# A hybrid encoder layer: early products read in place, rotary multiplications ordered behind the next job's first split, two norm products moved to VectorE

## The chip, the cores and the metric

The kernel runs on one core of a Trainium2 chip. The time is device microseconds from the start to the end of one execution; the figure of a kernel is the median of several executions. One execution is also recorded by the hardware profiler. Engines are named as in the profile: PE (TensorE: matmuls and transposes; PEld its weight loads), DVE (VectorE), ACT (ScalarE), POOL (GpSimd) and SP (SyncE, which here only issues transfers).

## The reference

One layer of an encoder trunk for 1024 tokens of width 1024, in float32:

```
x = x + 0.5 * norm(SwiGLU_1(norm(x)))                 # FFN 1, inner width 2816
u = norm(x);  rq, rk, rv, rg, nq, nk, nv, g_ret, g_na = split(u @ W_mix_in)
y_ret = (silu(rg) * headnorm(retention(rotary(rq), rotary(rk), rv))) @ W_ret_out
y_na  = neighbourhood_attention(nq, nk, nv) @ W_na_out
x = x + norm((sigmoid(g_ret) * y_ret + sigmoid(g_na) * y_na) @ W_mix_out)
x = x + 0.5 * norm(SwiGLU_2(norm(x)))                 # FFN 2
SwiGLU(x) = (silu(g) * up) @ w_out,  [g, up] = x @ w_in
rotary(x): [x1*cos - x2*sin, x1*sin + x2*cos], x1, x2 the halves of a head's 128 columns
norm(x) = x * rsqrt(mean(x*x) + 1e-6) * gain
```

## The kernel before

**Splitting.** A float32 matrix product is made of three matmuls on operands split in a high and a low part: `split` (L57) writes the high part with a cast on ACT (L62) and the low part with a subtraction on DVE (L63); `mm3` (L92) issues the three matmuls (L94, L95, L96; the third uses the low part of the stationary operand). Weight pieces come as `wraw` tiles of 128 x 1024 (four buffers, loaded through SP's queue, L73) and are split into `wh` and `wl` (eight buffers each).

**Pairs.** The large projections are done with a seven-product scheme (Strassen-Winograd) on pairs of weight tiles. One call of `Pairs.run` (L509) is a *job*: it loads the two tiles `g` and `u`, forms t1 to t4 from their halves on DVE (L525, L526, L536, L545), and makes the products p1, p6, p2, p7, p5, p4, p3 with the seven forms of x (`a11`, `s2`, `a12`, `s3`, `s1`, `a22`, `s4`). Every product is 12 matmuls into one PSUM bank. DVE adds the products up into four output tiles (`c11`, `c12`, `c21`, `c22`); `done(j)` is called when output j is complete.

**Early products.** The products of `a11` and `a12` need no t, so those of the first pairs are made before the jobs begin (`lead`, L460, and `leads`, L446). Of a *held* pair they stay in PSUM; of a *saved* pair (three in each FFN) `lead` copies both to SBUF tiles, named `lead` in FFN 1 and `g` in FFN 2, six buffers each. `run` then starts with a copy of p1 into the output tile c12 (L524) and adds p6 there (L535). In the FFNs c12 is the first half of a tile `gt` with three buffers, which `LeftFactors` (L577) later splits in place and stores to DRAM as `g0a`, `g0s` (FFN 1) or `g1a`, `g1s` (FFN 2); the stores are issued on POOL's queue (L69). FFN 1 makes the early products of a seventh pair as well, and leaves them in PSUM (tag `pt`).

**Mixer jobs.** Twelve pairs make the transposed outputs of the mixer's projection: four of neighbourhood q and k, then alternately a rotary job (rq and rk of a head; four in all) and a SiLU job (rg), then two sigmoid jobs. In a rotary job `done` calls `rotate` (L1048): two multiplications on DVE by the sine and cosine tables (L1051, L1052), a store, and two accumulating stores that swap the halves later.

**FFN output.** `ffn_out` (L689) does the seven products over 11 blocks each for 512 tokens and 512 columns at a time; a *step* is one block, 12 matmuls. When the product of `a22` ends, `p4` (L759) finishes tokens 0 to 3: the sum on DVE (L760), then `Epilogue.square` (L660): a sum of squares on ACT (L663) and a multiplication by the gain (L664), on POOL unless an engine is given. The rest of the two norms is cut into stages (`stages`, L764), which are appended to the list `later`; each following step takes one entry from its front: rstd (on POOL, L104), the residual (L674) with its sum of squares (L677), the second norm (L685), and the transposes on PE (`flip`, L133). FFN 2 has no second norm (`ep.pre` is None).

**Order.** Every engine and queue works in its own fixed order. A scheduler draws it up ahead of the run with a model of the durations: of the instructions that are ready by the model, the one written first goes first. A "NoSync" dependency (`after`, L76; `behind`, L503) fixes the order of two instructions on one engine.

Of the kernel before, what the change touches and what calls it, by code (L numbers as in the profile page):

```python
# [14 lines left out]
ALU = mybir.AluOpType  # L15
# [399 lines left out]
class Pairs:  # L415
# [2 lines left out]

    def __init__(self, c, x, srcs, held, saved=0):
        self.c, self.x, self.srcs, self.held, self.saved = c, x, srcs, held, saved  # L420
        self.begun, self.fetched, self.ready = {}, {}, {}
        self.last = None
        self.between = lambda: None

# [35 lines left out]
    def lead(self, save=None, between=(), on_pool=(), abreast=1, extra=0, early=False):  # L460

        def split(i):
            if i not in self.fetched:
                self.fetch(i)
            w = self.fetched[i]
            self.ready[i] = self.c.piece(w[:, :512])
            self.fetched[i] = [None, self.c.piece(w[:, 512:])]

        n = self.held + self.saved
        tiles = [i for i in (*range(self.held, n), *range(self.held), *range(n, n + extra)) if i not in self.begun]  # L470
        while tiles:
            group, tiles, abreast = tiles[:abreast], tiles[abreast:], 1
            for i in group:
                if i not in self.fetched:
                    self.fetch(i)
            g = [self.fetched.pop(i) for i in group]
            eng = self.c.nc.gpsimd if group[0] in on_pool else None
            tag = ("ps", 6) if group[0] < n else ("pt", 2)
            ps = [self.products("a11", [self.ready.pop(i) if i in self.ready else w[:, :512] for i, w in zip(group, g)],
                                eng, tag),  # L480
                  self.products("a12", [w[1] if isinstance(w, list) else w[:, 512:] for w in g], eng, tag)]
            if early and tiles:
                split(tiles[0])
            if between:
                f = between.pop(0)()
                if f is not None:
                    between.append(f)
            for i, *pair in zip(group, *ps):
                if self.held <= i < n:
                    sb = [save(), save()]  # L490
                    for a, b in zip(sb, pair):
                        for p, s in self.pieces(a):
                            self.c.nc.scalar.copy(p, b[:, s])
                    pair = sb
                self.begun[i] = pair

    @staticmethod
    def pieces(a):
        a = a if isinstance(a, list) else [a]
        n = 512 // len(a)  # L500
        return [(p, slice(j * n, (j + 1) * n)) for j, p in enumerate(a)]

    def behind(self, e):  # L503

# [1 line left out]
            self.c.tc.add_manual_dep(e.ins, self.last.name, mybir.DependencyInfo(  # L506
                mybir.DependencyClass.NoSync, mybir.DependencyReason.DATA), reason="order")

    def run(self, i, out, done):  # L509

        c, nc = self.c, self.c.nc
        tt = nc.vector.tensor_tensor
        g, u = (c.raw(a) for a in self.srcs[i])
        b11, b21, b12, b22 = g[:, :512], g[:, 512:], u[:, :512], u[:, 512:]

        t1, t3, t4 = b11, b12, b21
        t2 = c.wpool.tile([P, 512], F32, tag="t2", name="t2", bufs=2)

        begun = self.begun.get(i)
        p1 = begun[0] if begun else self.product("a11", b11)  # L520
        c11, c12 = out(0), out(2)
        u1 = c12 if begun else c11
        for p, s in self.pieces(p1):
            nc.scalar.copy(u1[:, s], p)  # L524
        self.behind(tt(t1, b12, b11, ALU.subtract))  # L525
        tt(t2, b22, t1, ALU.subtract)  # L526
        p6 = self.product("s2", t2)
        if not begun:
            tt(c12, p6, c11, ALU.add)
        p2 = begun[1] if begun else self.product("a12", b21)  # L530
        for p, s in self.pieces(p2):
            tt(c11[:, s], p, u1[:, s], ALU.add)  # L532
        done(0)
        if begun:
            tt(c12, p6, c12, ALU.add)  # L535
        self.behind(tt(t3, b22, b12, ALU.subtract))  # L536
        p7 = self.product("s3", t3)
        c21 = out(1)
        self.last = tt(c21, p7, c12, ALU.add).ins
        p5 = self.product("s1", t1)  # L540
        c22 = out(3)
        tt(c22, p5, c21, ALU.add)
        tt(c12, p5, c12, ALU.add)
        done(3)
        tt(t4, b21, t2, ALU.subtract)  # L545
        p4 = self.product("a22", t4)
        tt(c21, p4, c21, ALU.add)
        done(1)
        p3 = self.product("s4", b22)
        self.end = tt(c12, p3, c12, ALU.add).ins  # L550
        done(2)
# [137 lines left out]
def ffn_out(c, tiles, q, blocks, w_out, gl, ep, tail, side={}):  # L689
# [3 lines left out]
    nc = c.nc  # L693
    NK = FT // 2
    tt, add = nc.vector.tensor_tensor, nc.gpsimd.tensor_tensor
# [62 lines left out]

    def p4(u, b):  # L759
        tt(q[3][:, u], b, q[3][:, u], ALU.add)  # L760
        ep.square(u, 0, q[3][:, u], b)
        later.extend(stages(u, (q[3][:, u], q[2][:, u])))

    def stages(t, halves):  # L764
        g = ep.steps(t, xs[t], halves)

        f = []
        return [lambda: next(g), lambda: next(g)] + [
            lambda: f.append(next(g)), lambda: f[0](*(("ps", 6) if i < 6 else ("pt", 2)))] * (ep.pre is not None)

    def p2(u, b):
# [273 lines left out]
            nc.vector.tensor_scalar(q, q, RET_SCALE, None, ALU.mult)  # L1045


def rotate(c, t, x, cos, sin, dst):  # L1048

    tt = c.nc.vector.tensor_tensor  # L1050
    tt(t, x, sin, ALU.mult)  # L1051
    tt(x, x, cos, ALU.mult)  # L1052
    c.store(dst, x)

    def swap():
        c.nc.gpsimd.dma_start(dst[0:64], t[64:128], accum_op=ALU.add)
        c.nc.gpsimd.dma_start(dst[64:128], t[0:64], accum_op=ALU.add)
    return swap
# [159 lines left out]
def trunk_layer(ctx: ExitStack, tc, x, xt, g1a, w1i, w1o, g1b, gma, wmt, wnv, wrv, logits, dtab, rope, bias,  # L1218
                wro, wno, wmo, gmb, g2a, w2i, w2o, g2b, out):
    nc = tc.nc  # L1220
# [5 lines left out]
    c = Core(tc, const, wpool, psum, dram)  # L1226
# [29 lines left out]
    with tc.tile_pool(name="fin1", bufs=1, reuse_waits="tile") as fp:  # L1256
# [23 lines left out]
    ep = pool(ep_stack, "ep1")  # L1280
    g1 = pool(g_stack, "gl11")
    b11, b12, b21, b22 = ([p.tile([P, 4, 512], F32, tag="x", name="x", bufs=n) for p, n in q] for q in (
        ((x0pool, 4),) * 3, ((x1pool, 2), (x1pool, 2), (x0pool, 4)), ((spool, 8),) * 3, ((spool, 8),) * 3))
    q = [p.tile([P, 4, 512], F32, tag="x", name="q", bufs=n) for p, n in ((ep, 2), (ep, 2), (spool, 8), (spool, 8))]
# [72 lines left out]
    with tc.tile_pool(name="pa", bufs=1, reuse_waits="tile") as pa:  # L1357
        evpool[:] = [pa]
        fill.drain()
        swaps = []  # L1360

        def half():
            return pa.tile([P, 512], F32, tag="ev", name="ev", bufs=6)
# [6 lines left out]
        for i, (_, _, f, g, fn) in enumerate(jobs):  # L1370
# [6 lines left out]
            def done(j):  # L1377
                h = j % 2
                dst = (f, g)[j // 2][:, h * 512:(h + 1) * 512]
                while swaps:  # L1380
                    swaps.pop()()
                if fn == "rotary":
                    swaps.append(rotate(c, half(), parts[j], *tabs[h], dst))
                    return
                if fn is not None:
                    nc.scalar.activation(parts[j], parts[j], fn)
                c.store(dst, parts[j])
            mx.run(i, part, done)
            if i == 2:
                x1pool = pool(x1_stack, "x1b", "right")  # L1390
                a21[:] = [x1pool.tile([P, 4, 512], F32R, name=f"a21{q}") for q in "hl"]
# [251 lines left out]
```

## Time and profile before

| | |
|---|---|
| median of 3 runs | 2256.15 us (2255.41 to 2257.74) |
| the profiled execution | 2254.28 us, span 2252.5 us |
| PE busy | 2196.9 us, 98% of the span |
| DVE busy | 1637.6 us, 73% |
| ACT busy | 985.0 us, 44% |
| POOL busy | 581.7 us, 26% |
| granted TensorE clock, mean | 0.994 |

How to read the rows. In a timeline: start in us from the span's start, duration, engine, line, operation, output tile <- input tiles, shape, count of merged instructions, and in brackets how long the engine stood idle before it and what released it. Matmuls overlap, so their durations are longer than the distance of their starts. A row of waits gives who waited for whom, total us, number of times, longest. A row of the windows gives the busy time of each engine in a stretch of the span, then the granted clock as a share of full speed, the share of the DMA engines and GB/s.

### The profile page before, as it was taken

The numbers are of one execution on the slowest core, as the hardware profiler recorded it, in microseconds if no ns is written. First come the engines' busy times: TensorE is split into PE (matmuls) and PEld (weight loads), VectorE is DVE, ScalarE is ACT, GpSimd is POOL, SyncE is SP. The second block draws the span as 40 slices with busy tenths as digits, with TensorE's granted clock in tenths as the row PEclk, the third lists the DMA queues.
The fourth block names the chain that finished last, engine by engine and source line by source line (L and its number), as shares of the span: only waits on it lengthen the run. The fifth ranks groups of instructions, "written<-read, shape, count | busy, mean of one in ns | idle before, by whom it ended". The sixth has DMA issues, their size and how long they took to land.

```text
span 2252.5 us, 29976 instructions
## 1 busy us (share of the span) xinstructions
PE 2196.9 (98%) x10200; PEld 1824.7 (81%) x10200; DVE 1637.6 (73%) x2911; ACT 985.0 (44%) x2041; POOL 581.7 (26%) x756
## 2 busy tenths in 40 slices
PE   6899999999998999999999999999999999999998
PEld 5678888888786887888888888888887888888886
DVE  7898878765459857759885678553899887876444
ACT  5444434332345322249785665422544343433232
POOL 1121212158521112311101222111112121215942
PEclk9999999999999999999999999999999999999999
DMA  6354434497555555557665466686446443449865
GB/s 252 131 176 161 169 140 156 180 395 297 196 184 188 173 175 142 140 165 252 195 217 176 152 221 234 246 305 227 146 145 219 141 178 131 163 158 365 291 227 180
DMA packets 155464, 449.89 MB, mean 200 GB/s; under 512 B 19632, under 2 KB 50480, under 8 KB 153200
## 3 DMA queue, kind: packets, MB, share of 16 engines
q1 hardware_dynamic: 112800, 311.36, 40.9%
q0 software_dynamic: 42512, 136.62, 16.7%
q8 instruction: 81, 1.33, 0.2%
q14 instruction: 71, 0.58, 0.1%
HBM read 302.93 MB, written 149.17 MB: 201 GB/s over the span
## 4 chain that ended last, share of the span: by engine, by line
PE 82%; DVE 6%; ACT 4%; issue 4%; DMA 2%; POOL 2%; POOLq 0%; SPq 0%; DVEq 0%; ACTq 0%
PE ps L96 26%; PE ps L95 25%; PE ps L94 25%; PE pt L95 1%; PE pt L96 1%; PE pt L94 1%; POOL rstd L104 1%; ACT wh L62 1%; DMA wraw<-in_dram 1%; ACT s L937 1%; DVE wl L63 1%; DMA qraw<-nq 1%; DVE s L933 0%; PE pt L133 0%; ACT pth L62 0%
## 5 line engine op out<-in xcount | busy, mean ns | idle before, releaser
L63 DVE TENSOR_TENSOR wl<-wraw,wh 128x512 fp32r<-128x512 f32 x472 | 314.7, 683 | 61.0 <-ACT wh L62 60.7
L62 ACT CAST wh<-wraw 128x512 fp32r<-128x512 f32 x476 | 272.9, 618 | 159.3 <-PE ps L95 57.5
L94 PE MATMUL ps<-wh,g 128*128 128x512 f32 x548 | 214.1, 391 | 0.4 <-DVE tmp L231 0.4
L95 PE MATMUL ps<-wl,g 128*128 128x512 f32 x548 | 213.6, 390 | 0.0
L96 PE MATMUL ps<-wh,g 128*128 128x512 f32 x548 | 213.3, 389 | 0.0
L567 ACT ACTIVATE c<-c 128x512 f32<-128x512 f32 x88 | 55.4, 632 | 195.1 <-DVE c L532 101.6
L63 DVE TENSOR_TENSOR wl<-w,wh 128x512 fp32r<-128x512 f32 x77 | 77.0, 1018 | 86.2 <-ACT wh L62 86.0
L63 DVE TENSOR_TENSOR wl<-x,wh 128x512 fp32r<-128x512 f32 x77 | 79.7, 1051 | 75.1 <-ACT wh L62 73.7
L94 PEld LDWEIGHTS ps<-wh,g 128*128 128x128 f32 x548 | 102.9, 188 | 21.9 <-DVE tmp L231 0.7
L95 PEld LDWEIGHTS ps<-wl,g 128*128 128x128 f32 x548 | 102.9, 188 | 21.3 <-DVE wl L63 0.5
L96 PEld LDWEIGHTS ps<-wh,g 128*128 128x128 f32 x548 | 102.9, 188 | 21.3
L94 PE MATMUL ps<-a11h,wh 128*128 128x512 f32 x276 | 111.3, 403 | 7.7 <-ACT wh L62 7.7
L62 ACT CAST wh<-t 128x512 fp32r<-128x512 f32 x58 | 36.0, 621 | 184.0 <-DVE t L526 183.9
L96 PE MATMUL ps<-a11h,wl 128*128 128x512 f32 x276 | 109.6, 398 | 6.2 <-DVE wl L63 6.1
L95 PE MATMUL ps<-a11l,wh 128*128 128x512 f32 x276 | 109.9, 398 | 0.1
L96 PE MATMUL ps<-a22h,wl 128*128 128x512 f32 x280 | 109.1, 390 | 0.6 <-DVE wl L63 0.6
L94 PE MATMUL ps<-a22h,wh 128*128 128x512 f32 x280 | 109.7, 392 | 0.0
L94 PE MATMUL ps<-a12h,wh 128*128 128x512 f32 x276 | 108.7, 394 | 0.5 <-ACT wh L62 0.3
L95 PE MATMUL ps<-a22l,wh 128*128 128x512 f32 x280 | 109.1, 390 | 0.0
L95 PE MATMUL ps<-a12l,wh 128*128 128x512 f32 x276 | 107.5, 390 | 0.0
L96 PE MATMUL ps<-a12h,wl 128*128 128x512 f32 x276 | 107.5, 389 | 0.0
L94 PE MATMUL ps<-s2h,wh 128*128 128x512 f32 x232 | 91.8, 396 | 7.5 <-ACT wh L62 7.5
(427 smaller groups left out, 6287.2 us busy)
## 6 DMA issues: line engine op xcount, KB each, us to landing
wraw<-in_dram SPq DMA_DIRECT2D x204, 512.0 KB, 4.6
g<-g0s SPq DMA_DIRECT2D x44, 512.0 KB, 4.2
g<-g1s SPq DMA_DIRECT2D x44, 512.0 KB, 4.8
g<-g0a SPq DMA_DIRECT2D x33, 512.0 KB, 3.3
g<-g1a SPq DMA_DIRECT2D x33, 512.0 KB, 4.4
g0s<-gth POOLq DMA_DIRECT2D x44, 256.0 KB, 4.7
g0s<-cmb POOLq DMA_DIRECT2D x44, 256.0 KB, 3.7
g1s<-gth POOLq DMA_DIRECT2D x44, 256.0 KB, 4.7
```

The costliest lines, as they stand in the source:

```text
L62: self.done = [nc.scalar.copy(h, src).ins, (eng or nc.vector).tensor_tensor(l, src, hf, ALU.subtract).ins]
L63: (eng or nc.vector).tensor_tensor(l, src, hf, ALU.subtract).ins]
L94: mm(ps, a[0], b[0], start=start, stop=False)
L95: mm(ps, a[0], b[1], start=False, stop=False)
L96: mm(ps, a[1], b[0], start=False, stop=stop)
L104: self.nc.gpsimd.tensor_tensor(r[:, :n], ms, self.mhalf[:, :n], ALU.pow)
L567: nc.scalar.activation(gate[j], gate[j], AF.Silu)
L937: nc.scalar.activation(s[:, e], s[:, e], AF.Exp, bias=st[:, 2 + e:3 + e], accum_out=st[:, 4 + e:5 + e])
```

## The change

`lead` marks the saved pairs (`kept`) and copies each product whole. In `run`, a kept pair's p1 is read where it was saved: there is no copy into c12, and both additions take the saved tile. A job that is called with `nxt` loads the next job's `g` tile and splits its first half right after the product p5 is issued; the subtraction of that split is named `ahead`, and the next job uses the pieces (`ready`) instead of splitting anew. Rotary jobs set `nxt`, and the first multiplication of `rotate` for the outputs 3, 1 and 2 is ordered behind `ahead` on DVE. In `ffn_out` of FFN 1, the multiplication by the gain in `p4` is done on DVE for tokens 0 and 1, and an empty entry is put in front of token 0's last two stages in `later`. The helper `pieces` goes.

```diff
--- before.py
+++ after.py
@@ -418,7 +418,7 @@
 
     def __init__(self, c, x, srcs, held, saved=0):
         self.c, self.x, self.srcs, self.held, self.saved = c, x, srcs, held, saved
-        self.begun, self.fetched, self.ready = {}, {}, {}
+        self.begun, self.fetched, self.ready, self.kept = {}, {}, {}, set()
         self.last = None
         self.between = lambda: None
 
@@ -489,16 +489,10 @@
                 if self.held <= i < n:
                     sb = [save(), save()]
                     for a, b in zip(sb, pair):
-                        for p, s in self.pieces(a):
-                            self.c.nc.scalar.copy(p, b[:, s])
+                        self.c.nc.scalar.copy(a, b)
                     pair = sb
+                    self.kept.add(i)
                 self.begun[i] = pair
-
-    @staticmethod
-    def pieces(a):
-        a = a if isinstance(a, list) else [a]
-        n = 512 // len(a)
-        return [(p, slice(j * n, (j + 1) * n)) for j, p in enumerate(a)]
 
     def behind(self, e):
 
@@ -506,38 +500,42 @@
             self.c.tc.add_manual_dep(e.ins, self.last.name, mybir.DependencyInfo(
                 mybir.DependencyClass.NoSync, mybir.DependencyReason.DATA), reason="order")
 
-    def run(self, i, out, done):
+    def run(self, i, out, done, nxt=False):
 
         c, nc = self.c, self.c.nc
         tt = nc.vector.tensor_tensor
-        g, u = (c.raw(a) for a in self.srcs[i])
+        g = self.fetched.pop(i) if i in self.fetched else c.raw(self.srcs[i][0])
+        u = c.raw(self.srcs[i][1])
         b11, b21, b12, b22 = g[:, :512], g[:, 512:], u[:, :512], u[:, 512:]
 
         t1, t3, t4 = b11, b12, b21
         t2 = c.wpool.tile([P, 512], F32, tag="t2", name="t2", bufs=2)
 
         begun = self.begun.get(i)
-        p1 = begun[0] if begun else self.product("a11", b11)
+        p1 = begun[0] if begun else self.product("a11", self.ready.pop(i, b11))
         c11, c12 = out(0), out(2)
-        u1 = c12 if begun else c11
-        for p, s in self.pieces(p1):
-            nc.scalar.copy(u1[:, s], p)
+        u1 = p1 if i in self.kept else c12 if begun else c11
+        if u1 is not p1:
+            nc.scalar.copy(u1, p1)
         self.behind(tt(t1, b12, b11, ALU.subtract))
         tt(t2, b22, t1, ALU.subtract)
         p6 = self.product("s2", t2)
         if not begun:
             tt(c12, p6, c11, ALU.add)
         p2 = begun[1] if begun else self.product("a12", b21)
-        for p, s in self.pieces(p2):
-            tt(c11[:, s], p, u1[:, s], ALU.add)
+        tt(c11, p2, u1, ALU.add)
         done(0)
         if begun:
-            tt(c12, p6, c12, ALU.add)
+            tt(c12, p6, u1, ALU.add)
         self.behind(tt(t3, b22, b12, ALU.subtract))
         p7 = self.product("s3", t3)
         c21 = out(1)
         self.last = tt(c21, p7, c12, ALU.add).ins
         p5 = self.product("s1", t1)
+        if nxt:
+            self.fetch(i + 1)
+            self.ready[i + 1] = c.piece(self.fetched[i + 1][:, :512])
+            self.ahead = c.done[1].name
         c22 = out(3)
         tt(c22, p5, c21, ALU.add)
         tt(c12, p5, c12, ALU.add)
@@ -758,14 +756,15 @@
 
     def p4(u, b):
         tt(q[3][:, u], b, q[3][:, u], ALU.add)
-        ep.square(u, 0, q[3][:, u], b)
+        ep.square(u, 0, q[3][:, u], b, None, nc.vector if u < 2 and ep.pre is not None else None)
         later.extend(stages(u, (q[3][:, u], q[2][:, u])))
 
     def stages(t, halves):
         g = ep.steps(t, xs[t], halves)
+        wait = [None] * (t == 0 and ep.pre is not None)
 
         f = []
-        return [lambda: next(g), lambda: next(g)] + [
+        return [lambda: next(g), lambda: next(g)] + wait + [
             lambda: f.append(next(g)), lambda: f[0](*(("ps", 6) if i < 6 else ("pt", 2)))] * (ep.pre is not None)
 
     def p2(u, b):
@@ -1045,10 +1044,10 @@
             nc.vector.tensor_scalar(q, q, RET_SCALE, None, ALU.mult)
 
 
-def rotate(c, t, x, cos, sin, dst):
+def rotate(c, t, x, cos, sin, dst, behind):
 
     tt = c.nc.vector.tensor_tensor
-    tt(t, x, sin, ALU.mult)
+    c.after(tt(t, x, sin, ALU.mult).ins, behind)
     tt(x, x, cos, ALU.mult)
     c.store(dst, x)
 
@@ -1380,12 +1379,12 @@
                 while swaps:
                     swaps.pop()()
                 if fn == "rotary":
-                    swaps.append(rotate(c, half(), parts[j], *tabs[h], dst))
+                    swaps.append(rotate(c, half(), parts[j], *tabs[h], dst, [] if j == 0 else [mx.ahead]))
                     return
                 if fn is not None:
                     nc.scalar.activation(parts[j], parts[j], fn)
                 c.store(dst, parts[j])
-            mx.run(i, part, done)
+            mx.run(i, part, done, fn == "rotary")
             if i == 2:
                 x1pool = pool(x1_stack, "x1b", "right")
                 a21[:] = [x1pool.tile([P, 4, 512], F32R, name=f"a21{q}") for q in "hl"]
```

## The prediction

> **What bounds the kernel now.** I read the page first, then who TensorE (PE) waited for, then the timeline around each wait.
>
> ```profile
> span 2252.5 us, 29976 instructions
> ...
> PE 2196.9 (98%) x10200; PEld 1824.7 (81%) x10200; DVE 1637.6 (73%) x2911; ACT 985.0 (44%) x2041; POOL 581.7 (26%) x756
> ```
>
> ```profile
> PE ps L94 <- ACT wh L62: 15.5, 9, 5.1
> PE pt L348 <- POOL rstd L104: 12.7, 2, 11.0
> PE ps L96 <- DVE wl L63: 9.5, 6, 3.3
> PE ps L133 <- DVE q L685: 1.6, 1, 1.6
> ```
>
> TensorE is busy 98% of the span. The change removes no matmul, so it can only give time back where PE stands still or runs slowly: 2252.5 - 2196.9 = 55.6 us of idle, 12.7 of it at the start, which the change leaves alone. Three of the other waits lie exactly where the diff works, so the forecast is a sum of these three.
>
> **Part A, the copies of the early products.** This is FFN 1, at the end of a job (one run of the seven products of a pair). The rows come from the timeline of all engines:
>
> ```profile
> 104.62 0.39 PE L94 MATMUL ps<-s4h,wh 128*128 128x512 f32 x1
> ...
> 107.11 0.39 PE L96 MATMUL ps<-s4h,wl 128*128 128x512 f32 x1
> ...
> 108.73 0.62 ACT L524 COPY gt<-lead 128x512 f32<-128x512 f32 x1 [6.71 <-DMA g0a<-gt]
> ...
> 109.91 0.69 DVE L569 TENSOR_TENSOR gt<-c,gt 128x512 f32<-128x512 f32 x1 [2.92 <-ACT c L567]
> ...
> 111.12 0.68 DVE L526 TENSOR_TENSOR t<-wraw 128x512 f32<-128x512 f32 x1
> ...
> 111.89 0.62 ACT L62 CAST wh<-t 128x512 fp32r<-128x512 f32 x1 [0.64 <-DVE t L526]
> ...
> 112.56 0.80 PE L94 MATMUL ps<-s2h,wh 128*128 128x512 f32 x1 [5.06 <-ACT wh L62]
> ...
> 117.24 0.63 PE L95 MATMUL ps<-s2l,wh 128*128 128x512 f32 x1
> ...
> 118.02 0.40 PE L94 MATMUL ps<-s3h,wh 128*128 128x512 f32 x1
> ```
>
> The copy of a saved product (`lead`) into the gate tile (`gt`) stands 6.71 us in ACT's queue, because a store to DRAM (`g0a<-gt`) still reads that buffer. Behind it waits the SiLU (`c` L567), for that DVE's L569, behind that L526, for that the cast of `t`, and for that PE. Undisturbed, the twelve matmuls of s4 start within 107.11 - 104.62 = 2.49 us, 0.227 apart; 13 starts from 107.11 would reach 110.06, and the thirteenth came at 118.02. The loss is 7.96 us: the idle time, and matmuls of 0.63 us instead of 0.39 after it.
>
> The change drops these three copies per FFN (six of 0.62 us on ACT, which has room) and lets DVE read the saved tile, which lives on until P6's addition; each FFN has six such tiles for six saved products, so nobody waits for one. The first writer of that buffer becomes DVE's addition of P6, which comes only once PE has finished s2 of its own job. The blocked copy belongs to the job after the one that PE is about to start, so that addition comes more than a job later (its five products of 12 matmuls take 5 x 12 x 0.227 = 13.6 us), long after 108.73, and the wait is not handed to DVE.
>
> What is late next is `t`: DVE has its own backlog there. How much stays I take from two boundaries of the same kind, one later in FFN 1 and one in FFN 2:
>
> ```profile
> 141.73 0.59 ACT L524 COPY gt<-pt 128x512 f32<-128x512 f32 x1 [3.45 <-DMA g0a<-gt]
> ...
> 143.41 0.50 PE L94 MATMUL ps<-s2h,wh 128*128 128x512 f32 x1 [0.73 <-ACT wh L62]
> ```
>
> ```profile
> 1714.23 0.50 PE L94 MATMUL ps<-s2h,wh 128*128 128x512 f32 x1 [1.18 <-ACT wh L62]
> ...
> 1715.93 0.50 PE L96 MATMUL ps<-s2h,wl 128*128 128x512 f32 x1 [0.97 <-DVE wl L63]
> ```
>
> Each wait costs its idle time and 0.11 us for a longer first matmul (0.50 for 0.39): 0.84 us at the one, 1.18 + 0.97 + 0.22 = 2.37 us at the other. The mean is 1.6, so A gives 7.96 - 1.6 = 6.4 us. Upper end: all 7.96. Lower end, from DVE's room in the same jobs of the two FFNs:
>
> ```profile
> 93.50:173.70 80.20, 74.32 (x313) 59.83 (x312) 73.15 (x120) 32.49 (x57) 22.09 (x41) 0.96 0.58 205
> 1658.00:1731.00 73.00, 70.86 (x310) 57.71 (x309) 70.92 (x117) 31.36 (x55) 16.23 (x30) 1.00 0.54 195
> ```
>
> (Columns: window, PE, PEld, DVE, ACT, POOL busy, granted clock, DMA.) FFN 2 keeps DVE 70.92/73.0 = 97% busy. At that share DVE's 73.15 us in FFN 1 fill 75.3 us, which allows 80.2 - 75.3 = 4.9 us.
>
> A stall left behind may also cost clock (the number behind the POOL column):
>
> ```profile
> 107.10:118.00 10.90, 5.84 (x14) 3.97 (x13) 6.71 (x11) 5.18 (x9) 1.08 (x2) 0.69 0.42 167
> 865.20:872.10 6.90, 4.51 (x13) 3.28 (x13) 6.39 (x10) 2.18 (x4) 4.60 (x6) 0.76 0.75 131
> ```
>
> ```profile
> 1712.50:1716.50 4.00, 1.86 (x7) 0.91 (x6) 4.00 (x8) 1.87 (x3) 0.54 (x2) 1.00 1.05 383
> ```
>
> The stall in FFN 2 (two waits of about 1 us) kept the full granted clock, that of part B (2.39 us at 868.24) had 0.76. The Trainium skill's "TensorE: Matmul & The Clock Gate" (Why this matters for your kernels) lets the clock drop only after gaps above about 3 us. By that page the remainder stays at 1.6 us and A at 6.4; by the row at 868.24 it grows by the 1.6 us of slow matmuls there (4.2 less 2.4 less 0.2) and A is 4.8. The 0.76 after 2.39 us speaks against the page's figure.
>
> In FFN 2 the same three copies hold nobody up for long (PE's stall there has DVE work behind it), so I count 0, between 2.4 gained (that stall goes) and 2.4 lost (it doubles).
>
> **Part B, rotary.** The second rotary job ends and the next job begins:
>
> ```profile
> 851.50 0.62 ACT L62 CAST wh<-wraw 128x512 fp32r<-128x512 f32 x1
> ```
>
> ```profile
> 865.44 0.69 DVE L550 TENSOR_TENSOR ev<-ps,ev 128x512 f32<-128x512 f32 x1 [0.57 <-PE ps L96]
> 865.47 0.39 PE L95 MATMUL ps<-a11l,wh 128*128 128x512 f32 x1
> ...
> 866.89 0.69 DVE L1052 TENSOR_TENSOR ev<-ev,tab 128x512 f32<-128x512 f32 x1
> ...
> 867.50 0.68 DVE L63 TENSOR_TENSOR wl<-wraw,wh 128x512 fp32r<-128x512 f32 x1
> ...
> 868.22 0.69 DVE L525 TENSOR_TENSOR wraw<-wraw 128x512 f32<-128x512 f32 x1
> ...
> 868.24 0.50 PE L96 MATMUL ps<-a11h,wl 128*128 128x512 f32 x1 [2.39 <-DVE wl L63]
> ...
> 869.73 0.62 ACT L62 CAST wh<-t 128x512 fp32r<-128x512 f32 x1 [17.60 <-DVE t L526]
> ...
> 872.18 0.44 PE L94 MATMUL ps<-s2h,wh 128*128 128x512 f32 x1
> ```
>
> The high half was cast at 851.50, yet the subtraction for `wl` sits behind the rotary multiplications. From 865.47 to 872.18 are 6.71 us for 11 starts, 2.50 us at 0.227: 4.2 us lost. The change moves one SP load, one cast and this subtraction ahead; the load's data had landed by 851.50, so SP's queue is no matter. POOL's stores of the rotated halves follow the multiplications and so go one subtraction, 0.7 us, later; no wait of PE in the list above hangs on them. With `wl` gone from 867.50, L525 starts there, the cast of `t` 0.72 earlier at 869.0, and s2 at 869.7, where PE would want it at 867.97: 1.7 us stay, B gives 2.5. If DVE does L525 right after L539, as at the next rotary boundary, nothing stays:
>
> ```profile
> 889.39 1.89 DVE L63 TENSOR_TENSOR wl<-wraw,wh 128x512 fp32r<-128x512 f32 x3
> ...
> 899.66 0.69 DVE L539 TENSOR_TENSOR ev<-ps,ev 128x512 f32<-128x512 f32 x1 [0.58 <-PE ps L96]
> 900.27 0.68 DVE L525 TENSOR_TENSOR wraw<-wraw 128x512 f32<-128x512 f32 x1
> ```
>
> I can't tell the two orders apart and take the middle, 3.4 us. The other three rotary boundaries have no PE wait to give back: 0.
>
> **Part C, two products on DVE.** End of FFN 1's output stage:
>
> ```profile
> 608.28 3.00 POOL L664 TENSOR_TENSOR q<-q,gain 128x512 f32<-128x512 f32 x2 [13.71 <-ACT ps L663]
> ...
> 611.84 3.47 DVE L674 SCALAR_TENSOR_TENSOR x<-q,rstd,x 128x512 f32<-128x512 f32 x2 [1.72 <-POOL rstd L104]
> ...
> 616.99 1.41 DVE L685 SCALAR_TENSOR_TENSOR q<-x,rstd,gain 128x512 f32<-128x512 f32 x2 [0.67 <-POOL rstd L104]
> ...
> 617.89 1.29 PE L133 MATMUL ps<-ident,q 128*128 128x128 f32 x8 [1.55 <-DVE q L685]
> ```
>
> The first transposes come 1.55 us late (1.7 with the longer start). Two POOL products (3.00 us) leave the path; DVE takes 1.4 us (0.7 each, as L685) to 3.5 us (1.7 each, as L674 beside POOL), with L674 of token 0 behind them. The added empty step puts the transposes 12 matmuls, 2.7 us, later in PE's order: more than the stall, even if the data came no sooner. The transposes of tokens 1 to 3 move by one step too; none of them shows in the list of PE's waits. FFN 2's output stage has no second norm and keeps its code. C gives 1.7; lower end 0.
>
> **Sum.** 6.4 + 3.4 + 1.7 = 11.5 us off. Against the profiled run's own 2254.28 us (span 2252.5) that is 2242.8; the median of the runs, 2256.15, lies 1.87 above that run, so the forecast is 2244.7. Its own range: gains from 4.9 + 2.5 + 0 - 2.4 = 5.0 to 8.0 + 4.2 + 1.7 + 2.4 = 16.3, or 2239.9 to 2251.2.
>
> **Rivals.**
> - The wait moves to the copy that stays. L524 `gt<-pt` (141.73) is not dropped and waits 3.45 us for a store. If PE arrives 6.4 us earlier and DVE's backlog keeps the store where it is, that wait takes about 4 back. For it: DVE at 97%. Against it: the stores follow DVE work that is freed too. A = 2.4, in all 2.4 + 3.4 + 1.7 = 7.5: 2248.7.
> - The rotary edit does not do what it says: the scheduler still puts `wl` late, since the cast was ready 16 us before and was passed over. B = 0, in all 8.1: 2248.1.
> - The planner's new order gives it back: both of these (2.4 + 1.7 = 4.1 gained), and another boundary that now costs as much as the mean of the two above (1.6) or a little more: 2253.7.
> - Slower: the rotary multiplications, held behind `wl`, gather at job boundaries. Six of 0.65 us ahead of L525 are 3.9 us. At this boundary `wl` would follow L550 (866.1 to 866.8, PE 1.2 us late), L525 come at 870.7, s2 2.2 us later at 872.9, where the a11 product is through at 869.2: 3.7 us, and 2.4 us of slow clock (12 matmuls, 0.2 each). That is 1.2 + 3.7 + 2.4 - 4.2 = 3.1 more than before, and 6.1 at each of the three boundaries that now lose nothing, 21.4 us. Less A and C (8.1) it ends 13.3 slower: 2269.5. It decides once L525 starts under 2.2 us (its own time, L526, the cast) before the a11 product ends. Against it: at 889.39 `wl` is split a whole job ahead.
>
> **Chances.** Forecast 0.54, moved wait 0.16, rotary edit idle 0.12, given back 0.10, slower 0.08. This kernel's measurement separates about 0.2% (4.5 us): faster means below 2251.6. The first three fall there but for about 0.06, so faster 0.76, same 0.16, slower 0.08. The range 2239.5 to 2252.5 holds the first three whole and leaves out most of the last two.
>
> **What would show it.** A: no copy from `lead` on ACT, PE's 5.06 us wait gone, the next one at that boundary under 2.5 us, granted clock of that stretch back near 1. B: `wl` ahead of the last multiplications, no wait on it at the second rotary job's end, L525's place telling 2.5 from 4.2. C: two L664 rows on DVE, no wait of PE on L685. Wrong would be a longer wait at the `gt<-pt` copy, or s2 waiting for L526 after each rotary job.

## The result, and the profile after

On one chip the changed kernel takes 2251.69 us (median of 19 runs) and the kernel before 2255.51 us (of 20). The ratio of the two is put at 0.9981, 95% interval 0.9973 to 0.9988, or -4.3 us (-6.1 to -2.7). A single run of 3438 us here, and one above 3100 us in each of two experiments, were disturbed and are not counted. The forecast was -11.5 us, 2244.7: the direction was right, the size was not, by 7 us.

The profiled run of the changed kernel took 2244.99 us, almost exactly the forecast and 9.3 us less than the profiled run of before. It misleads: it is the fastest of the runs, 7 us under their median. Why one profile can be so far off is answered by the rows on the granted clock below.

From the page of the changed kernel, and its list of PE's waits (us in total, times, longest):

```profile
span 2243.2 us, 29960 instructions
...
PE 2192.1 (98%) x10200; PEld 1820.9 (81%) x10200; DVE 1635.0 (73%) x2913; ACT 982.3 (44%) x2035; POOL 577.5 (26%) x754
```

```profile
PE pt L348 <- POOL rstd L104: 13.0, 2, 10.9
PE ps L94 <- ACT wh L62: 11.6, 7, 3.7
PE ps L96 <- DVE wl L63: 10.1, 8, 3.3
```

The wait on L685 (part C) has left the list, the waits for casts are 3.9 us shorter (part A), and the waits for low parts, which part B was to shorten by 2.4 us, are not shorter: 10.1 us for 9.5.

Line numbers of the changed kernel are a few lower: L520, L521 are the first two subtractions of a job, L526 the sum c11, L545 and L548 the sums after a22 and s4, L567 the product with up, L540 and L541 the sums after s1, L1050 and L1051 the rotary multiplications, L662 the norm product, L683 the last scaling.

**Part A.** The same boundary in the timeline of the changed kernel, PE, DVE and ACT:

```profile
103.47 0.68 DVE L545 TENSOR_TENSOR c<-ps,c 128x512 f32<-128x512 f32 x1
104.07 0.68 DVE L520 TENSOR_TENSOR wraw<-wraw 128x512 f32<-128x512 f32 x1
104.67 0.69 DVE L526 TENSOR_TENSOR c<-lead 128x512 f32<-128x512 f32 x1
105.27 0.68 DVE L567 TENSOR_TENSOR gt<-c,gt 128x512 f32<-128x512 f32 x1
105.47 0.39 PE L96 MATMUL ps<-s4h,wl 128*128 128x512 f32 x1
105.90 0.69 DVE L548 TENSOR_TENSOR gt<-ps,gt 128x512 f32<-128x512 f32 x1
106.50 0.68 DVE L521 TENSOR_TENSOR t<-wraw 128x512 f32<-128x512 f32 x1
107.28 0.62 ACT L62 CAST wh<-t 128x512 fp32r<-128x512 f32 x1 [0.67 <-DVE t L521]
107.95 0.50 PE L94 MATMUL ps<-s2h,wh 128*128 128x512 f32 x1 [2.09 <-ACT wh L62]
109.05 0.50 PE L96 MATMUL ps<-s2h,wl 128*128 128x512 f32 x1 [0.37 <-DVE wl L63]
```

No copy from `lead` stands on ACT any more. The 5.06 us wait is 2.09 + 0.37 us. What is left is DVE's own backlog: three operations (L526, L567, L548) stand between L520 and L521, which makes `t`. By the prediction's way of counting (starts against 0.227 us each), this place lost 7.96 us and in this profile loses 3.0 us.

**Part B.** The second rotary job in the same timeline, with the row of DVE's low parts in the kernel before after it:

```profile
843.65 1.66 ACT L62 CAST wh<-wraw 128x512 fp32r<-128x512 f32 x3
...
852.12 0.69 DVE L540 TENSOR_TENSOR ev<-ps,ev 128x512 f32<-128x512 f32 x1 [2.03 <-PE ps L96]
852.38 0.39 PE L94 MATMUL ps<-s4h,wh 128*128 128x512 f32 x1
852.73 0.68 DVE L541 TENSOR_TENSOR ev<-ps,ev 128x512 f32<-128x512 f32 x1
853.33 0.68 DVE L63 TENSOR_TENSOR wl<-wraw,wh 128x512 fp32r<-128x512 f32 x1
853.93 0.69 DVE L1050 TENSOR_TENSOR ev<-ev,tab 128x512 f32<-128x512 f32 x1
854.53 0.68 DVE L63 TENSOR_TENSOR wl<-wraw,wh 128x512 fp32r<-128x512 f32 x1
855.13 0.69 DVE L1051 TENSOR_TENSOR ev<-ev,tab 128x512 f32<-128x512 f32 x1
855.27 0.50 PE L96 MATMUL ps<-a22h,wl 128*128 128x512 f32 x1 [2.50 <-DVE wl L63]
855.73 0.69 DVE L63 TENSOR_TENSOR wl<-wraw,wh 128x512 fp32r<-128x512 f32 x1
```

```profile
850.11 1.29 DVE L63 TENSOR_TENSOR wl<-wraw,wh 128x512 fp32r<-128x512 f32 x2 [0.16 <-ACT wh L62]
```

The next job's first split is now ahead of the multiplications, as the change says, and its a11 product no longer waits. But all three casts were done by 845.3 (843.65 + 1.66), and all three low parts follow only after the sums of s1. In the kernel before, the two of this job's own a22 and s4 were made at 850.11, right behind their casts. Now they stand behind the early one, so this job's a22 product waits 2.50 us. A wait of 2.39 us went, one of 2.50 us came two products earlier.

**Part C.** DVE and PE at the end of FFN 1's output stage:

```profile
601.03 1.28 DVE L662 TENSOR_TENSOR q<-q,gain 128x512 f32<-128x512 f32 x2
...
608.93 1.42 DVE L683 SCALAR_TENSOR_TENSOR q<-x,rstd,gain 128x512 f32<-128x512 f32 x2 [0.67 <-POOL rstd L104]
...
611.38 1.04 PE L133 MATMUL ps<-ident,q 128*128 128x128 f32 x8
```

The two products take 1.28 us on DVE where POOL took 3.00, and the flips start without a wait. By an estimate from these rows the empty step is needed for that: 12 matmuls (2.7 us) earlier, at 608.7, the first of the two results of L683 was not ready (608.93 + 0.71). No run has one of the two edits without the other.

### The profile page after: what moved, and what is told of

Same layout as the page of the kernel before. It is cut to its first block, busy times and chain, and to the rows that moved or that the text cites. A ratio compares the mean times of both kernels' runs of the same rounds, so it can differ in the third digit from the quotient of the medians.

```text
span 2243.2 us, 29960 instructions
## 1 busy us (share of the span) xinstructions
PE 2192.1 (98%) x10200; PEld 1820.9 (81%) x10200; DVE 1635.0 (73%) x2913; ACT 982.3 (44%) x2035; POOL 577.5 (26%) x754
## 4 chain that ended last, share of the span: by engine, by line
PE 83%; DVE 6%; issue 4%; ACT 4%; DMA 2%; POOL 1%; POOLq 0%; SPq 0%; DVEq 0%; ACTq 0%
PE ps L96 26%; PE ps L95 26%; PE ps L94 26%; PE pt L94 1%; PE pt L95 1%; PE pt L96 1%; POOL rstd L104 1%; DVE wl L63 1%; DVE s L932 1%; ACT wh L62 1%; DMA qraw<-nq 1%; DMA wraw<-in_dram 0%; ACT s L936 0%; PE pt L133 0%; DVE ptl L63 0%
## 5 line engine op out<-in xcount | busy, mean ns | idle before, releaser
L62 ACT CAST wh<-w 128x512 fp32r<-128x512 f32 x77 | 46.6, 620 | 110.9 <-PE pt L96 56.6
```

The costliest lines, as they stand in the source:

```text
L62: self.done = [nc.scalar.copy(h, src).ins, (eng or nc.vector).tensor_tensor(l, src, hf, ALU.subtract).ins]
```

## The experiments

The kernel before is timed beside every run; us are the ratio's distance from 1 times 2255. Jobs are numbered from 0 to 13 (four of q and k, eight alternating, two sigmoid: fourteen pairs, not twelve), so that the rotary jobs are 4, 6, 8 and 10, and the wait above sits between 6 and 7.

**The three parts alone, and the whole once more.** Each of the first three leaves the other two parts as before.

*p_copies* is the changed kernel with these lines taken back, and without the moved norm products:

```
-   swaps.append(rotate(c, half(), parts[j], *tabs[h], dst, [] if j == 0 else [mx.ahead]))
+   swaps.append(rotate(c, half(), parts[j], *tabs[h], dst, []))
...
-   mx.run(i, part, done, fn == "rotary")
+   mx.run(i, part, done)
```

> Part A alone (the saved pairs' products read in place; the rotary order and the norm products as before). Theory (a stall is worth its idle time, and the slow clock that may follow it is no fixed part of it): the stall of 5.06 us at the boundary of the pairs 2 and 3 (107 us) shrinks to about 2.1 us, that at 142 us (1.4 us) goes: ratio near -4 us, between -3 and -5.5 us against the kernel before. Rival (the prediction's price, with 2.5 us of slow clock counted as part of the stall): -6.4 us. The wait of 2.4 us ahead of the a11 product at the boundary of the jobs 6 and 7, and the one of 2.0 us ahead of the flip at 616 us, stay.

Measured: ratio 0.998 (0.9971 to 0.9989), -4.5 us (-6.5 to -2.5). The waits at this boundary are again 2.09 and 0.37 us. The theory's value holds. The rival's -6.4 lies just inside the interval, so the time alone doesn't exclude it; the losses counted in the profiles (below) speak against it.

*p_rotary* is the changed kernel without `self.kept.add(i)` and without the moved norm products.

> Part B alone (the next job's first split ahead of the rotary multiplications; the copies and norm products as before). Theory: the wait of 2.4 us ahead of the next job's a11 product goes, but the job's own a22 product then waits about 2.5 us for its low part on VectorE, since the low parts of t4 and b22 are ordered behind the early split: ratio within 1 us of the kernel before. Rival (the prediction): -3.4 us, with no wait of over 1 us near 850 to 870 us.

Measured: 1.0007 (0.9998 to 1.0017), +1.6 us (-0.5 to +3.8). PE in its timeline:

```profile
866.08 0.50 PE L96 MATMUL ps<-a22h,wl 128*128 128x512 f32 x1 [2.50 <-DVE wl L63]
```

The wait moved as in the whole change, and the part alone brings nothing.

*p_norms* is the kernel before with the two edits of part C alone.

> Part C alone (two norm products on VectorE and one more place in the list of flips). Theory: the wait of 2.0 us ahead of the flip at 616 us goes and nothing takes its place: -2 us, between -1.2 and -2.4 us. Rival: the wait had covered work that is now late elsewhere near 620 to 690 us: within 0.7 us of the kernel before.

Measured: 0.9989 (0.998 to 0.9997), -2.5 us (-4.5 to -0.7), and no wait at the flips.

*all_again* is the changed kernel itself.

> The changed kernel again, for a second profile of it on another occasion. Theory: the same idle times at the same places (2.1 us near 107 us, 2.5 us near 853 us, none near 616 us), but TensorE at a low granted clock behind other stalls than in the first profile, and a time of 0.3 to 0.5% over that profile's 2245 us; -4 to -6 us against the kernel before, about the sum of the three parts alone. Rival (the low clock belongs to the stall and goes with it): the places of low clock are the same as in the first profile of the changed kernel, and the span is within 1 us of its 2243.2 us.

Measured: 0.9976 (0.9968 to 0.9985), -5.4 us (-7.2 to -3.4); the three parts alone make -4.5 + 1.6 - 2.5 = -5.4 as well. Its profiled run took 2252.60 us, 7.6 us more than the first one of the same kernel. The idle times are the same to the hundredth (2.09, 0.37, 2.50); the granted clock behind them is not. Windows of 8.6 and 7.7 us from the last matmul ahead of each wait (the number behind the POOL column is the clock), first profile, then second:

```profile
105.40:114.00 8.60, 6.15 (x27) 4.44 (x26) 8.60 (x15) 4.74 (x8) 1.08 (x2) 1.00 0.54 219
852.30:860.00 7.70, 5.20 (x24) 3.97 (x23) 7.53 (x13) 2.16 (x4) 1.96 (x3) 1.00 0.72 189
```

```profile
107.30:115.90 8.60, 6.15 (x20) 4.27 (x19) 7.38 (x13) 4.09 (x7) 1.08 (x2) 0.80 0.51 203
859.00:866.70 7.70, 5.20 (x16) 3.79 (x15) 7.25 (x12) 2.18 (x4) 1.91 (x3) 0.78 0.71 181
```

In the 8.6 us with the same waits, PE does 27 matmuls at full clock and 20 at 0.80: 7 x 0.227 = 1.6 us. So the slow clock is no fixed part of a stall of this length; it differs from execution to execution.

**Where the a22 wait comes from.** *late_split* gives the early load and split out one product later, behind a22 in place of s1 (lines are shortened):

```
         p4 = self.product("a22", t4)
+        if nxt:
+            self.fetch(i + 1)
+            self.ready[i + 1] = c.piece(self.fetched[i + 1][:, :512])
+            self.ahead = c.done[1].name
...
-   ... dst, [] if j == 0 else [mx.ahead]))
+   ... dst, [] if j in (0, 3) else [mx.ahead]))
```

> The changed kernel, with job 7's early load and first split given out after the a22 product is given out, not ahead of it (so that the low part of t4 is split as before, and that of b22 is not). Theory: the wait of 2.5 us ahead of a22 at 853 us goes and stands ahead of the s4 product instead, a product (2.8 us) later: VectorE gives the sum after a22, the early low part, a multiplication and then s4's low part, four operations of 0.6 us, so a wait of 1.6 to 2.2 us; time within 1.5 us of the changed kernel's, -4 to -7 us against the kernel before. Rival (the split's place in the order does not matter, the casts on ScalarE do): the wait is ahead of a22 as before, 2.5 us.

PE and DVE in its timeline:

```profile
857.55 0.69 DVE L545 TENSOR_TENSOR ev<-ps,ev 128x512 f32<-128x512 f32 x1
858.15 0.68 DVE L63 TENSOR_TENSOR wl<-wraw,wh 128x512 fp32r<-128x512 f32 x1
858.75 0.68 DVE L1050 TENSOR_TENSOR ev<-ev,tab 128x512 f32<-128x512 f32 x1
859.35 0.69 DVE L63 TENSOR_TENSOR wl<-wraw,wh 128x512 fp32r<-128x512 f32 x1
860.10 0.50 PE L96 MATMUL ps<-s4h,wl 128*128 128x512 f32 x1 [1.91 <-DVE wl L63]
```

The four operations stand as expected, and s4 waits 1.91 us in a22's place. The time is 0.9971 (0.996 to 0.9982), -6.5 us, not to be told from the changed kernel's. So the place of the split in DVE's order sets which product waits, and moving the split only moves the wait.

**Why job 6 and no other.** The other three rotary jobs have no such wait, with the same code. What is special about job 6 is SP's queue in the kernel before:

```profile
814.04 2.45 SPq L1402 DMA_DIRECT2D nvg<-nv  x4
838.29 0.93 SPq L73 DMA_DIRECT2D wraw<-in_dram  x2
```

Four gathers of stored results (DRAM to DRAM, for a later stage) stand ahead of job 7's two loads (838.29). On the chip they cost SP 2.45 us and that load is in time: its cast runs at 851.50, 16 us ahead of the subtraction that PE waits for (867.50). The theory was that the scheduler's model takes them for long, believes job 7's load late, and so places job 7's first split late on DVE. *late_gathers_b* is the kernel before with the gathers ordered behind the last load (lines are shortened):

```
+            if i == len(jobs) - 1:
                 for cb in range(4):
-                    nc.sync.dma_start(d["nvg"][cb]...
+                    e = nc.sync.dma_start(d["nvg"][cb]...
+                    c.after(e.ins, [c.fetch.name])
```

> The kernel before, with the four gathers nvg<-nv taken off their place on SP's queue (ahead of job 7's first load) and ordered behind the last job's load; nothing else. Theory: the planner takes these four transfers for long, puts job 7's load and first split late in its order, and the rotary multiplications of job 6 slip ahead of that split on VectorE; with the gathers elsewhere the split stands ahead of them and the 2.4 us wait at 866 us ahead of the a11 product goes, no wait at a22 or s4 in its place: -2.4 us, up to -4 with the slow clock that follows it in some runs. Rival: the multiplications stand ahead of the split for their own cost, wherever the gathers are: the wait stays, 0 us.

*best_v1* has the copies' and the norm products' parts as well, and no rotary part.

> The changed kernel without its rotary part (no early split, no order) but with the four gathers ordered behind the last job's load. Theory: no wait of over 1 us from 840 to 880 us, neither ahead of a11 nor of a22; with the copies' and the norm products' parts (-4.5 and -2.3 us alone) and 2.4 us for the wait: -9 us, between -7.5 and -11 us against the kernel before. Rival: a wait turns up at the first reads of nvg, at about 1000 us, since the gathers come late: -6 us or less.

Measured: 1.0022 (1.0013 to 1.0032), +5.0 us, and 0.9999 (0.999 to 1.0008), -0.2 us. Both parts of the expectations came true at once: neither kernel has a wait near 866 us, and both have a new one at the start of the next stage. ACT and PE of best_v1:

```profile
996.26 1.31 ACT L65 ACTIVATE qh<-qraw 128x256 fp32r<-128x256 f32 x4
997.48 2.28 ACT L62 CAST k<-kraw 64x512 fp32r<-64x512 f32 x4
999.78 2.18 ACT L62 CAST wh<-wraw 128x512 fp32r<-128x512 f32 x4
1000.45 1.22 PE L94 MATMUL ps<-wh,a11h 128*128 128x512 f32 x2 [5.50 <-ACT wh L62]
```

ACT's order around the start of that stage is another one now: the casts for q and k stand ahead of the weights that PE needs, 5.50 us late. In the kernel before, ACT casts weights at 984.61 to 991.97 us, ahead of q and k (1004.28). It is the rival's place, but the wait is for a cast, not for `nvg`.

*spread_gathers* is the changed kernel with the gathers given out at job 11 and not ordered; they then stand singly behind each pair of loads.

> The changed kernel with the four gathers given out at the end of job 11 and free to go where the planner finds SP idle: one stands ahead of each of the loads of jobs 7, 8, 9 and so on. Theory: what matters is where the planner puts a gather ahead of a load that a rotary job's early split needs; job 6 is now free of it and its a22 wait at 853 us goes, but job 8 has one ahead of job 9's load, and its a22 product, at about 890 us, gets the wait instead, 2.0 to 2.5 us: -4 to -7 us against the kernel before, as the changed kernel. Rival: the wait is job 6's own (its place behind job 3's long chain on VectorE), so it stays at 853 us or goes without a successor.

```profile
894.36 0.50 PE L96 MATMUL ps<-a22h,wl 128*128 128x512 f32 x1 [0.61 <-DVE wl L63]
...
918.82 0.50 PE L94 MATMUL ps<-a11h,wh 128*128 128x512 f32 x1 [1.95 <-ACT wh L62]
```

The wait at 853 us is gone and job 8 has one ahead of its a22, as expected in place, but of 0.61 us only: PE's own order had more matmuls of the next products in front there. A second one, 1.95 us, I had not foreseen: the a11 product of job 10 waits for its cast, which ACT makes only behind job 9's last activation. 0.9971 (0.996 to 0.9982), -6.5 us. So the gathers' places move the waits, but one gather ahead of a load doesn't make a wait by itself: SP's queue has one ahead of job 7's load as well (gather at 807.72, load at 825.60), and job 6 has no wait.

*act_gathers_b* and *best_v2* leave the gathers where they are in the program and issue them from ACT's queue: `nc.scalar.dma_start(d["nvg"][cb]...` for `nc.sync.dma_start`. The first is the kernel before, the second has the copies' and norm products' parts and no rotary part.

> The kernel before, with the four gathers nvg<-nv issued from ScalarE's queue at the same place of the program, not from SP's; nothing else. Theory: SP's queue is then the loads alone, the planner has job 7's first split early, and the wait of 2.4 us ahead of a11 at 866 us goes, while the loads at the start of the next stage (at about 1000 us) stay in their order, so that the 5.5 us wait that the late gathers brought there does not come: -2.4 us, up to -4 with the slow clock. Rival: ScalarE waits for the stores of nv ahead of the gathers and its casts come late: a new wait of PE for a cast near 815 us, 0 to +4 us.

> The changed kernel without its rotary part (no early split, no order), with the gathers on ScalarE's queue. Theory: the copies' and norm products' parts (-4.5 and -2.3 us alone) and the rotary wait (-2.4) add up: -9 us, between -7.5 and -11. Rival: as for the run before: -5 us or less.

ACT and PE of act_gathers_b:

```profile
814.35 2.46 ACTq L1402 DMA_DIRECT2D nvg<-nv  x4
835.06 0.58 ACT L524 COPY ev<-ps 128x512 f32<-128x512 f32 x1 [22.99 <-DVE ev L1051]
...
836.22 0.80 PE L94 MATMUL ps<-s2h,wh 128*128 128x512 f32 x1 [5.73 <-ACT wh L62]
```

1.0025 (1.0015 to 1.0035), +5.6 us, and 0.999 (0.998 to 1.0), -2.3 us. The rival won, with another releaser than it named: the wait at 866 us is gone, but ACT stands idle 23 us ahead of a copy that needs a buffer of the rotary halves, with the next job's casts behind it, and PE waits 5.73 us. The copy itself is no later than in the kernel before (835.07 there); what changed is ACT's order, which there has the cast of `t` ahead of it, at 821.30.

*best_v3* adds to best_v2 that t1, t2 and the split of t2 of the next pair are given out inside the job before, behind a22 and s4:

```
         p4 = self.product("a22", t4)
+        if i + 1 in self.begun:
+            g, u = (c.raw(a) for a in self.srcs[i + 1])
+            self.early[i + 1] = g, u, self.firsts(g, u)
...
         p3 = self.product("s4", b22)
+        if i + 1 in self.early:
+            self.ready[i + 1] = c.piece(self.early[i + 1][2])
```

> As the run before, and in both FFN stages the next pair's first two subtractions (t1, t2) are given out behind the a22 product of the pair before, and the split of t2 behind its s4 product, so that both stand on VectorE ahead of that pair's last sums and products with up. Theory: what is left of the wait at the boundary of the pairs 2 and 3 (2.1 us at 107 us) and the waits at 170 us (1.4 us) and 1711 us (2.7 us) are the same thing, t2 queued on VectorE behind the pair before's last operations, and go: a further -4 to -6 us, -13 to -15 us against the kernel before. Rival: the wait is for the weights or for ScalarE's cast, not for VectorE's order: it stays, -9 us.

Measured: 0.9991 (0.9982 to 1.0), -2.0 us: nothing over best_v2. The waits for t2 at 107, 170 and 1711 us did go. In their place the s3 product waits for its cast: 0.56 us at 109, 2.36 at 139 and 2.96 at 1715 us. From 93.5 to 173.7 us DVE is busy 77.29 of 80.20 us in this run, and what was put first on it made the next operand late.

**The gathers on POOL's queue**, `nc.gpsimd.dma_start(d["nvg"][cb]...`: in the kernel before (*pool_gathers_b*), with the copies' and norm products' parts and no rotary part (*best_v4*), and in the whole changed kernel (*pool_gathers_all*).

> The kernel before, with the four gathers nvg<-nv issued from POOL's queue, behind the stores of nv that they read. Theory: the 2.4 us wait ahead of a11 at 866 us goes, as in both runs that took the gathers off SP; POOL has only stores behind them, which wait some 5 us longer, and the buffers of the rotary halves come free in time, so that no cast waits as ScalarE's did (23 us ahead of job 5's copy) and the loads at 1000 us keep their order: -2.4 us, between -1 and -4. Rival: the stores of the halves come late behind the gathers, and the copy of a later job's c11 waits for its buffer with PE behind it near 835 us: +3 to +6 us, as with ScalarE's queue.

> The changed kernel without its rotary part (no early split, no order), with the gathers on POOL's queue. Theory: copies -4.5, norm products -2.5, the rotary wait -2.4: -9 us, between -7 and -11. Rival: as for the run before: -3 us or less.

> The whole changed kernel, rotary part too, with the gathers on POOL's queue. Theory: the early split was only harmful because the planner had job 7's load late; with the load early the order asks nothing of VectorE, the a22 wait at 853 us goes as well, and this is as fast as the run before: -7 to -11 us. Rival: the early split takes the low parts of t4 and b22 behind it whatever the gathers do: a22 waits 2 to 2.5 us again, -5 us.

Measured, in this order: 0.998 (0.9971 to 0.9989), -4.5 us; 0.9962 (0.9948 to 0.9976), -8.6 us; 0.9964 (0.9951 to 0.9977), -8.1 us. The first gains more than the 1 to 4 us expected, though the interval (-6.5 to -2.5) reaches into them. Windows, DVE and POOL of best_v4, where L1046 is the first multiplication, L524 the sum c11 and L1397 the gathers:

```profile
840.00:880.00 40.00, 40.00 (x177) 32.87 (x176) 32.18 (x52) 14.12 (x25) 12.49 (x18) 1.00 0.57 151
```

```profile
810.66 1.99 POOL L1397 DMA_DIRECT2D nvg<-nv  x4 [4.15 <-DMA nv<-ev]
...
849.75 1.90 DVE L63 TENSOR_TENSOR wl<-wraw,wh 128x512 fp32r<-128x512 f32 x3
851.57 0.69 DVE L526 TENSOR_TENSOR ev<-ps,ev 128x512 f32<-128x512 f32 x1
852.29 0.69 DVE L1046 TENSOR_TENSOR ev<-ev,tab 128x512 f32<-128x512 f32 x1
```

Over the whole of the stretch PE is busy 40.00 of 40.00 us. All three low parts, those of a22, s4 and the next job's a11, are made at 849.75, ahead of the first multiplication, with no order written for it. POOL stands 4.15 us for the stores that the gathers read. DVE waits for a store of POOL's queue once between 805 and 880 us (`rk<-ev`, 5.5 us), but PE has no wait there. With the rotary part added the time is the same within the intervals: no gain and no cost of the part shows there. best_v4 has the lowest ratio of all kernels timed (in 5 runs), below the changed kernel's 0.9981 and 0.9976; it was not timed beside the changed kernel itself, and the intervals overlap.

That moving the gathers removes the waits is shown: the one at a11 on SP's, ACT's and POOL's queue, the one at a22 on SP's and POOL's. That it does so because the model of the scheduler overrates these transfers is argued from the order, not shown: no run changed the model, and these moves changed the order of other instructions too.

## Why the prediction was right or wrong

**Part B's term failed: a gain of 3.4 us predicted, +1.6 us (-0.5 to +3.8) measured, that is no gain.** The step that failed is "The change moves one SP load, one cast and this subtraction ahead". It followed the subtraction that had been late and asked only what came after it (L525, the cast of `t`, s2). It did not ask what the early split is put in front of. On DVE that was the low parts of the same job's t4 and b22, made at 850.11 in the kernel before and at 854.53 and 855.73 in the changed one. Both ends of its range, 2.5 and 4.2 us, take it for granted that no other product waits; the a22 product now waits 2.50 us. The rival "the rotary edit does not do what it says" had B = 0 right, for another reason: the edit does order the split ahead. "The planner's new order gives it back" came nearest with its sum, 2.5 us gained: a wait did turn up elsewhere, but by the order that the edit itself asks for, and its A = 2.4 rested on a wait at the `gt<-pt` copy that didn't come. The slower rival named this place's other danger (multiplications gathered at the boundary); that did not come.

**Part A's mechanism was right, its size too large by the profiles: 6.4 us predicted, 4.5 (2.5 to 6.5) measured.** The blocked copy was the cause, it went, nothing handed the wait to p6's addition, and `t` behind DVE's backlog was late next, as said. What stays was put at 1.6 us, from two other boundaries. It is 2.09 + 0.37 us idle with longer first matmuls, 3.0 us, and 4.6 us where the clock drops: in six of the nine profiles that have this very boundary. By 7.96 less 3.0 or 4.6 the place gives 5.0 or 3.4 us. The prediction had worked out 4.8 us for a remainder with slow clock, from its row at 868.24, but its sum kept 6.4. The boundary of the `gt<-pt` copy shrank as well (0.73 us of wait to 0.19), so the rival that sent the wait there is out. FFN 2's wait stayed (1.18 + 0.97 us in the kernel before, 1.18 + 0.97 after), as the 0 said:

```profile
1704.90 0.50 PE L94 MATMUL ps<-s2h,wh 128*128 128x512 f32 x1 [1.18 <-ACT wh L62]
1706.60 0.50 PE L96 MATMUL ps<-s2h,wl 128*128 128x512 f32 x1 [0.97 <-DVE wl L63]
```

**Part C was right**: 1.7 us predicted, 2.5 (0.7 to 4.5) measured alone, and the wait is gone.

**The clock.** The prediction took 7.96 and 4.2 us as the worth of the two stalls, slow matmuls included, because one profile showed them. For the first this held: all six profiles with that stall have the slow clock. For the rotary stall, 2.39 us of idle time with its low clock, two later profiles with the same idle time (p_copies, p_norms) lost 2.7 us. Its 1.6 us of slow clock were the chance of one execution.

**The sum.** Of the 7.2 us between -11.5 and -4.3, B makes 3.4 + 1.6 = 5.0 and A 1.9; C gave 0.8 more than counted, and the remaining 1.1 us lies within the intervals. The range, 2239.5 to 2252.5, held the median of 2251.69 near its end; that is luck in part, since it was drawn for the forecast and for rivals that end at 2248 to 2249, not for a wait that the edit itself makes. The prediction gave a chance of 0.76 to a time below 2251.6, and the median lies just above.

## What to carry to other kernels

When an instruction is ordered earlier on an engine, list what it overtakes and who waits for those, not only who waited for it; an order edit on a full engine tends to move a wait by one product (a11, a22, s4, s3 here). When one instance of a loop stalls and its identical siblings don't, look for what only that instance has, in every queue: here four transfers in SP's order, and moving them to POOL's queue removed the 2.4 us wait that an order written by hand only moved. Price a stall by its idle time, and count the slow clock that may follow as a chance, from several profiles.

## What the runs showed that I had not expected

The granted clock after a stall differs between executions. Grouped by wait, with the loss counted as in the prediction (a wait written as a sum is two waits with a few matmuls between them):

- 5.06 to 5.49 us (the kernels with the copies, 107 us): low clock in 6 of 6 profiles, loss 7.96 to 8.20 us.
- 3.28 to 3.37 us (the mixer's first products, 709 to 718 us, in every kernel): 3.6 us in 6 profiles, 5.2 to 6.1 in 10.
- 2.09 + 0.37 us (the same place as the first without the copies): 3.0 us in 3 profiles, 4.5 to 4.6 in 6.
- 2.38 to 2.50 us (the rotary job, a11 or a22): 2.7 to 2.8 us in 3, 4.2 to 4.4 in 3.
- 1.18 + 0.97 us (FFN 2, 1711 us): 2.7 us in 11 profiles, 4.2 to 4.3 in 4.

So slow clock follows the shortest of these waits in 4 of 15 profiles and the longest in all 6; between them, from 2.4 to 3.3 us, the counts (3 of 6, 6 of 9, 10 of 16) are too few to tell the lengths apart, and the 1.91 us of late_split had it in its only profile. With half a dozen such places the differences add up to several us: the two profiles of the changed kernel, with mean granted clocks of 0.996 and 0.993, are 2243.2 and 2250.8 us long with the same waits at the places above. The wait of 3.32 us alone makes 2.4 of these 7.6 us; windows of 8.6 us from the last matmul ahead of it, first profile, then second:

```profile
705.50:714.10 8.60, 5.28 (x24) 4.05 (x22) 8.60 (x16) 1.95 (x4) 0.00 (x0) 1.00 0.30 87
```

```profile
709.70:718.30 8.60, 5.28 (x14) 3.84 (x13) 8.60 (x16) 1.97 (x4) 0.00 (x0) 0.65 0.33 79
```

The Trainium skill's "TensorE: Matmul & The Clock Gate" (What's actually happening) says that the activity window of about 3.4 us runs freely, and that the number of slow matmuls at a kernel's start therefore varies from run to run. The counts above, for stalls inside a kernel, agree with that: in the windows around the 3.32 us wait PE did 24 matmuls in one profile and 14 in the other. The Trainium skill's rule for a gap on the same page (Why this matters for your kernels), above about 3 us, is no sharp bound here: waits of 2.09 + 0.37 us were followed by a clock of 0.80 (second profile of the changed kernel) as well as 1.00 (first), and the waits of 3.28 to 3.37 us by full clock in 6 of 16 profiles.
